# Hybrid RWKV-7 and attention layer: the block inverses work on a compact tile that ScalarE gathers, with one transposition in place of four

## The chip, the cores and the metric

The kernel runs on one core of one Trainium2 chip. The metric is device time in microseconds of one execution; the lower the better. The engines are named as in the profile: PE (TensorE, with PEld its weight loads), DVE (VectorE), ACT (ScalarE), POOL (GpSimd) and SP (SyncE, which here only issues DMAs). Each serves its own instructions in order.

## What is computed

One layer of a streaming encoder, on 512 prompt tokens and 32 sample tokens: a joint input projection, differential attention beside RWKV-7 time mixing, a merge with an output projection, and a gated ConvFFN. The part that matters here is the RWKV-7 recurrence, in the reference a loop over tokens:

```python
def step(S, inp):
    r_t, w_t, k_t, v_t, kk_t, a_t = inp
    sa = jnp.einsum('bhvk,bhk->bhv', S, -kk_t)
    S = (S * w_t[:, :, None, :] + sa[..., None] * (kk_t * a_t)[:, :, None, :]
         + v_t[..., None] * k_t[:, :, None, :])
    y = jnp.einsum('bhvk,bhk->bhv', S, r_t)
    return S, y
```

There are 16 heads of 64 values. The kernel does it in chunks of 64 tokens. Inside a chunk the tokens depend on each other through a unit triangular 64x64 matrix per head and chunk, and its inverse is needed before the chunks can be walked through.

## The kernel before

All large products are dense projections. `dense_g` (L222) makes one output tile of 128 columns: weights come by DMA in pieces of 128x512 (`load_w`, L212: L217 the DMA into one of three raw buffers `wr`, L218 the cast to `wh` on ACT, L219 the rest `wl` on DVE or POOL), and three matmuls of 272 columns per piece of 128 rows go into a PSUM tile `psd`. In the first stage these projections (first those that the recurrence needs, then fillers for the attention and the gates) fill TensorE between the small steps of the recurrence.

`Flow.run` (L106) puts the streams into one program: generators yield a time of a rough TensorE clock at which they want to go on, and dense work is taken while none is ready. Behind it a scheduler with costs of its own sets the final order on each engine, so a change of durations in the program text moves instructions far beyond the lines that it touches. The order on an engine is fixed when the program is built.

The streams of the first stage are:
- `elementwise` (L1059): per pair of heads, the decay and key terms (`rw_rates`, `rw_elem`, with norm products over `bonesr` into PSUM tiles `misc`, emptied by L565 and L587), stored to DRAM as `ar_d` and `bk_d`;
- `recurrence` (L1064): for each of two groups of four pairs, `rw_super` (L659) and then `rw_chain` (L720), which walks through the 8 chunks;
- `norms` (L1071) behind each chain (`rw_norm`, L841, with L867 and L871 emptying PSUM), `rw_sample` (L918) for the sample tokens, and `rotary`.

Behind these comes the attention (`attention`, L1297), with what is left of the fillers and the next projections as dense work beside it, and then dense stages to the end.

`rw_super` works on 32 small matrices for each of two heads. For each pair `chunk_products` (L615) makes the products and masks them into `mt` (L626), a tile of 128 partitions x 2 heads x 32 matrices x 128 columns. The 32x32 diagonal blocks lie in four quadrants of 32 partitions, each at a head and a column offset of its own; `QUADS` (L606) lists them. In turn:
1. L675: DVE transposes each quadrant's blocks into `NP` (a 32x32 blockwise transposition of 32x1024 elements), four instructions;
2. `inverse` (L480): 15 steps of a triangular inverse on the 16x16 diagonal blocks, two DVE instructions each, over 128 partitions, result in `Xp`;
3. `join16` (L631) joins 16x16 to 32x32 blocks: L635 transposes four quadrants of `Xp` into `NP`; `spread` (L680) transposes four quadrants of `Xp` to their places in `XT`; 128 matmuls, L645 empties them on ACT, 128 more, and L656 puts the result into `XT` on ACT and DVE in turn;
4. the join of 32x32 to 64x64 blocks: L688 transposes two quadrants of `XT` into `NP`, 64 matmuls, L698 empties them, 64 more, L708 puts them into `XT`.

`rw_chain` reads `mt` and `XT`. Its `load` (L728) brings `arL` and `bkL`, two buffers each, which `load_arbk` (L608) uses for the products too. A tile of such a name that is asked for takes the oldest buffer, and whatever writes it waits for the last reader of the tile before. `misc` has two PSUM buffers that all these steps share.

Of the kernel before, what the change touches and what calls it, by code (L numbers as in the profile page):

```python
# [10 lines left out]
F32 = mybir.dt.float32  # L11
# [15 lines left out]
SEQ = 512  # L27
# [9 lines left out]
SUP = 4  # L37
C = 64
NC = SEQ // C
# [122 lines left out]
def tile_hybrid_layer(  # L162
# [25 lines left out]
    V, A, G = nc.vector, nc.scalar, nc.gpsimd  # L188
    PE = Issue(tc, nc.tensor)
# [170 lines left out]
    rs, ms, rt = [npool.tile([128, TOK], F32, name=n) for n in ("rs", "ms", "rt")]  # L360
# [13 lines left out]
    for k in range(KT):  # L374
# [14 lines left out]
        for t in range(2):  # L389
            wh, wl = ws[t]  # L390
            for hf, (c0, c1) in enumerate(HALVES):
                for ip, (w, x) in enumerate(((wh, xg_h), (wh, xg_l), (wl, xg_h))):
                    PE.matmul(pj[t][hf][:, :c1 - c0], w[:, k % WK, :], x[:, k, c0:c1],
                              start=(k == 0 and ip == 0), stop=(k == KT - 1 and ip == 2))
# [59 lines left out]
    rp = ph1.enter_context(tc.tile_pool(name="rp", bufs=1, reuse_waits="tile"))  # L454
# [4 lines left out]
    def misc():  # L459
        return psm.tile([128, 512], F32, name="misc")  # L460


    mt = rp.tile([128, 2, 32, 128], F32, name="mt")
    XT = rp.tile([128, 32, 64], F32, name="XT")
# [5 lines left out]
    Xp = Xf[:, 0:1024].rearrange("p (a i) -> p a i", i=32)  # L470
    G.memset(XT, 0.0)

    def diag16(flat):

        return flat.rearrange("p (u x) -> p u x", u=2)[:, :, 0:512].rearrange("p u (a w) -> p u a w", w=32)[:, :, :, 0:16]

    def new_np():
        return rp.tile([128, 1056], F32, name="NP")

    def inverse(npf):  # L480

        X, N = diag16(Xf), diag16(npf)
        for i in range(1, 16):
            if i == 1:
                V.tensor_copy(out=X[:, :, 0, 1], in_=N[:, :, 1, 0])
                continue
            tmp = rp.tile([128, 512], F32, name="itmp")
            tv = tmp[:, :2 * i * i].rearrange("p (u a j) -> p u a j", u=2, a=i)
            V.tensor_tensor(out=tv, in0=X[:, :, 0:i, 0:i],
                            in1=N[:, :, i, 0:i].unsqueeze(2).to_broadcast([128, 2, i, i]), op=ALU.mult)  # L490
            V.tensor_reduce(out=X[:, :, 0:i, i], in_=tv, axis=AX.X, op=ALU.add)
# [114 lines left out]
    QUADS = [(32 * b + 64 * (1 - h), b, h) for h in range(2) for b in range(2)]  # L606

    def load_arbk(p):  # L608
        a = rp.tile([128, 2, SEQ], F32, name="arL", bufs=2)
        b = rp.tile([128, NC, 2, C], F32, name="bkL", bufs=2)  # L610
        nc.sync.dma_start(out=a, in_=ar_d[p, :, :, 0:SEQ])
        nc.sync.dma_start(out=b, in_=bk_d[p])
        return a, b

    def chunk_products(dst, m0, a, b):  # L615

        for q in range(NC // 4):
            pm = [misc(), misc()]
            for i in range(4):
                c = 4 * q + i  # L620
                for h in range(2):
                    f = slice(h * 64, h * 64 + 64)
                    PE.matmul(pm[h][:, i * 128:(i + 1) * 128], b[f, c, :, :].rearrange("p a t -> p (a t)"),
                              a[f, :, c * C:(c + 1) * C], start=True, stop=True)
            for h in range(2):
                V.tensor_tensor(out=dst[:, h, m0 + 4 * q:m0 + 4 * q + 4, :],  # L626
                                in0=pm[h].rearrange("p (m k) -> p m k", m=4),
                                in1=mask.unsqueeze(1).to_broadcast([128, 4, 128]), op=ALU.mult)
            yield PE.now + 2.0

    def join16(rows, src, M, xt, wait, spread):  # L631

        xz = new_np()[:, 0:512].rearrange("p (m a) -> p m a", m=32)
        for r0 in rows:
            V.transpose(out=xz[r0:r0 + 32].rearrange("p m a -> p a m"), in_=Xp[r0:r0 + 32, 0:16, :])  # L635
        spread()
        yield PE.now + wait
        ps = misc()
        for m in range(M):
            for q, r0 in enumerate(rows):  # L640
                PE.matmul(ps[r0:r0 + 32, m * 16:(m + 1) * 16], src(q, m), xz[r0:r0 + 32, m, :], start=True, stop=True)
        w = rp.tile([128, 512], F32, name="itmp")
        n = M * 16
        if len(rows) == 4:
            A.copy(out=w[:, :n], in_=ps[:, :n])  # L645
        else:
            for r0 in rows:
                A.copy(out=w[r0:r0 + 32, :n], in_=ps[r0:r0 + 32, :n])
        yield PE.now + 1.2
        ps = misc()  # L650
        for m in range(M):
            for q, r0 in enumerate(rows):
                PE.matmul(ps[r0:r0 + 16, m * 16:(m + 1) * 16], w[r0:r0 + 32, m * 16:(m + 1) * 16],
                          xt(q, slice(r0, r0 + 32))[:, m, 16:32], start=True, stop=True)
        for q, r0 in enumerate(rows):
            (V.tensor_copy if q % 2 else A.copy)(out=xt(q, slice(r0, r0 + 16))[:, 0:M, 16:32],  # L656
                                                 in_=ps[r0:r0 + 16, :n].rearrange("p (m k) -> p m k", m=M))

    def rw_super(s):  # L659
        p0 = s * SUP  # L660
        ab = {}
        for jj in range(SUP):
            yield ("out", p0 + jj), 0.0
            for k in range(jj, min(jj + 2, SUP)):
                if k not in ab and ("out", p0 + k) in flow.done:
                    ab[k] = load_arbk(p0 + k)
            yield max(PE.now + (4.0 if jj == 0 else 0.0), flow.done["out", p0 + jj] + 12.0)
            yield from chunk_products(mt, jj * NC, *ab[jj])
        yield from lock()


        with tc.high_priority(offset=1500):
            npf = new_np()
            for r0, b, h in QUADS:
                V.transpose(out=npf[r0:r0 + 32, 0:1024],  # L675
                            in_=mt[r0:r0 + 32, h, :, 32 * b:32 * b + 32].rearrange("p m t -> p t m"))
            inverse(npf)
        def spread():
            for r0, b, h in QUADS:
                V.transpose(out=XT[r0:r0 + 32, :, 32 * b:32 * b + 32].rearrange("p m i -> p i m"),  # L680
                            in_=Xp[r0:r0 + 32].rearrange("p a i -> p i a"))
        yield from join16(
            [q[0] for q in QUADS],
            lambda q, m: mt[QUADS[q][0]:QUADS[q][0] + 32, QUADS[q][2], m, 32 * QUADS[q][1]:32 * QUADS[q][1] + 32], 32,
            lambda q, r: XT[r, :, 32 * QUADS[q][1]:32 * QUADS[q][1] + 32], 28.0, spread)
        xz = new_np()[:, 0:1024].rearrange("p (m a) -> p m a", m=32)
        for r0 in (0, 64):
            V.transpose(out=xz[r0:r0 + 32], in_=XT[r0:r0 + 32, :, 0:32])  # L688
        yield PE.now + 7.0
        for m0 in (0, 16):  # L690
            ps = misc()
            for m in range(m0, m0 + 16):
                for h in range(2):
                    r0 = 64 * (1 - h)
                    PE.matmul(ps[r0 + 32:r0 + 64, (m - m0) * 32:(m - m0 + 1) * 32], mt[r0:r0 + 32, h, m, 32:64],
                              xz[r0:r0 + 32, m, :], start=True, stop=True)
            for r0, e in ((0, A.copy), (64, V.tensor_copy)):
                e(out=xz[r0 + 32:r0 + 64, m0:m0 + 16, :], in_=ps[r0 + 32:r0 + 64].rearrange("p (m k) -> p m k", m=16))  # L698
        yield PE.now + 1.5
        for m0 in (0, 16):  # L700
            ps = misc()
            for m in range(m0, m0 + 16):
                for h in range(2):
                    r0 = 64 * (1 - h)
                    PE.matmul(ps[r0:r0 + 32, (m - m0) * 32:(m - m0 + 1) * 32], xz[r0 + 32:r0 + 64, m, :],
                              XT[r0 + 32:r0 + 64, m, 32:64], start=True, stop=True)
            for r0, e in ((0, A.copy), (64, V.tensor_copy)):
                e(out=XT[r0:r0 + 32, m0:m0 + 16, 32:64], in_=ps[r0:r0 + 32].rearrange("p (m k) -> p m k", m=16))  # L708
        unlock()

    def lock():

        while flow.lock is not None:
            yield PE.now + 0.5
        flow.lock = True

    def unlock():
        flow.lock = None
# [199 lines left out]
    def rw_sample():  # L918
# [50 lines left out]
        def spread():  # L969
            V.transpose(out=xts.rearrange("p m i -> p i m"), in_=Xp.rearrange("p a i -> p i a"))  # L970
        yield from join16([0, 64], lambda q, m: mts[B[q], m, 0:32], 8, lambda q, r: xts[r], 26.0, spread)
        unlock()
        yield PE.now + 1.0
# [442 lines left out]
    with tc.tile_pool(name="op", bufs=1) as op:  # L1416
# [16 lines left out]
        ms, rt = [op.tile([128, TOK], F32, name=n) for n in ("ms", "rt")]  # L1433
# [11 lines left out]
    with tc.tile_pool(name="up", bufs=1) as up:  # L1445
# [11 lines left out]
        for f in range(FT):  # L1457
            cc = []
            for i in range(2):
                t = 2 * f + i  # L1460
# [23 lines left out]
    with tc.tile_pool(name="yp", bufs=1) as yp, tc.tile_pool(name="wlast", bufs=6, side="right") as wlast:  # L1484
        x2 = yp.tile([128, KT, TOK], F32, name="x2")
        acc = yp.tile([128, TOK], F32, name="acc")
        ms, rt, rs2 = [yp.tile([128, TOK], F32, name=n) for n in ("ms", "rt", "rs2")]
# [181 lines left out]
```

## Time and profile before

| | |
|---|---|
| median of 3 runs | 1366.93 us (1361.94 to 1367.68) |
| the profiled execution, its own time | 1367.84 us |
| its span, first to last instruction | 1366.0 us |
| mean granted TensorE clock over the span | 0.952 of 2.4 GHz |
| PE, PEld busy | 93%, 88% |
| DVE, ACT, POOL busy | 63%, 42%, 17% |
| first and second inverse, from L675 to the end of the joins | 210 to 288 us, 413 to 472 us |

The profile is one execution. A row of the trace gives the start, the duration, the engine, the line, the operation and the tiles (out<-in), and in brackets how long the engine had stood idle and which instruction released it. The share of busy time is a mean over stages with different limits, so the rows of the stage itself are read, and within it the wait that ends last. A TensorE row's busy time overlaps with the next one's, so the rate of dense matmuls is read from their starts.

### The profile page before, as it was taken

Reading aid. Unit: us, or ns where it says so; the run is one execution under the profiler, and the core shown is the slowest. Engines: PE = TensorE matmul, PEld = TensorE weight load, DVE = VectorE, ACT = ScalarE, POOL = GpSimd, SP = SyncE. Lnnn points to the kernel's source line nnn. Section 1 sums busy time; section 2 is a strip of 40 time slices with the busy share of each in tenths; the row PEclk is TensorE's granted clock in tenths of the full one; section 3 lists DMA queues with packets and bytes.
Section 4 is the critical chain, followed back from the end, with each engine's and each line's share of the span. In section 5 each row is a group of like instructions: output and inputs, shape, how many; then the busy total and the mean of one; then the engine's idle time right before and its main releaser. Section 6 shows DMA issues by size and latency. Waiting matters only on the chain. (4 is left out here: it accounts for less than half of the span.)

```text
span 1366.0 us, 29766 instructions
## 1 busy us (share of the span) xinstructions
PE 1264.7 (93%) x12014; PEld 1201.0 (88%) x12014; DVE 860.2 (63%) x1742; ACT 575.9 (42%) x1168; POOL 229.1 (17%) x264
## 2 busy tenths in 40 slices
PE   8798998799989899999987997999999999999996
PEld 7698988688878899988775895999999999999996
DVE  6857669855679333753456666566787777873323
ACT  5555454464412233332454555334544444453220
POOL 6600102111223101222221110000111111111111
PEclk9899898899989899999998998999999999999998
DMA  5254565144676253526776563345222222234321
GB/s 174 77 163 146 151 206 156 64 145 135 200 232 199 76 152 118 173 94 208 223 206 187 152 169 95 102 153 166 86 91 87 86 90 89 86 116 137 102 79 66
DMA packets 140329, 185.75 MB, mean 136 GB/s; under 512 B 42016, under 2 KB 65184, under 8 KB 140192
## 3 DMA queue, kind: packets, MB, share of 16 engines
q1 hardware_dynamic: 127120, 162.60, 39.9%
q10 hardware_dynamic: 13072, 21.26, 4.7%
q8 instruction: 94, 1.54, 0.5%
q14 instruction: 43, 0.35, 0.1%
HBM read 133.54 MB, written 37.41 MB: 125 GB/s over the span
## 5 line engine op out<-in xcount | busy, mean ns | idle before, releaser
L218 ACT CAST wh<-wr 128x512 fp32r<-128x512 f32 (+1 forms) x316 | 192.4, 615 | 374.2 <-PE psd L88 322.7
L88 PE MATMUL psd<-h_h,wh 128*128 128x272 f32 x976 | 299.5, 307 | 5.0 <-ACT qt L888 4.7
L88 PE MATMUL psd<-h_h,wl 128*128 128x272 f32 x976 | 291.7, 300 | 2.0 <-POOL wl L219 2.0
L88 PE MATMUL psd<-h_l,wh 128*128 128x272 f32 x976 | 292.7, 300 | 0.2 <-DVE h_l L443 0.2
L219 DVE TENSOR_TENSOR wl<-wr,wh 128x512 fp32r<-128x512 f32 x230 | 158.4, 693 | 116.9 <-ACT wh L218 111.9
L88 PEld LDWEIGHTS psd<-h_h,wh 128*128 128x128 f32 x976 | 192.9, 198 | 12.7 <-ACT qt L888 5.6
L88 PE MATMUL psd<-xgh,wl 128*128 128x272 f32 x704 | 203.9, 290 | 0.0
L88 PE MATMUL psd<-xgl,wh 128*128 128x272 f32 x704 | 203.3, 289 | 0.0
L88 PE MATMUL psd<-xgh,wh 128*128 128x272 f32 x704 | 202.1, 287 | 0.0
L88 PEld LDWEIGHTS psd<-h_h,wl 128*128 128x128 f32 x976 | 192.6, 198 | 4.3 <-POOL wl L219 2.5
L88 PEld LDWEIGHTS psd<-h_l,wh 128*128 128x128 f32 x976 | 193.2, 198 | 2.9 <-issue 1.4
L219 POOL TENSOR_TENSOR wl<-wr,wh 128x512 fp32r<-128x512 f32 x86 | 120.1, 1401 | 399.6 <-ACT wh L218 335.4
L88 PEld LDWEIGHTS psd<-xgl,wh 128*128 128x128 f32 x704 | 132.6, 188 | 0.0
L88 PEld LDWEIGHTS psd<-xgh,wl 128*128 128x128 f32 x704 | 132.4, 188 | 0.0
L88 PEld LDWEIGHTS psd<-xgh,wh 128*128 128x128 f32 x704 | 132.1, 188 | 0.1
L88 PE MATMUL psd<-ah,wh 128*128 128x272 f32 x352 | 101.7, 289 | 0.0
L88 PE MATMUL psd<-ah,wl 128*128 128x272 f32 x352 | 101.5, 288 | 0.0
L88 PE MATMUL psd<-al,wh 128*128 128x272 f32 x352 | 101.4, 288 | 0.0
L88 PE MATMUL psd<-ml,wh 128*128 128x272 f32 x256 | 74.6, 291 | 0.9 <-POOL ml L1134 0.9
L88 PE MATMUL psd<-mh,wh 128*128 128x272 f32 x256 | 74.8, 293 | 0.5 <-ACT mh L1133 0.4
L88 PE MATMUL psd<-mh,wl 128*128 128x272 f32 x256 | 74.6, 292 | 0.0
L1467 POOL COPY cvo<-uf 128x2 f32<-128x2 f32 x88 | 37.0, 452 | 220.6 <-DVE uf L1464 220.6
(369 smaller groups left out, 2537.5 us busy)
## 6 DMA issues: line engine op xcount, KB each, us to landing
wr<-w_in SPq DMA_DIRECT2D x132, 256.0 KB, 3.2
wr<-w_up SPq DMA_DIRECT2D x88, 256.0 KB, 2.8
wr<-w_down SPq DMA_DIRECT2D x40, 256.0 KB, 2.7
bkL<-bk_d SPq DMA_DIRECT2D x16, 512.0 KB, 5.2
ar_d<-ar SPq DMA_DIRECT2D x8, 544.0 KB, 3.2
t_d<-qt ACTq DMA_DIRECT2D x16, 272.0 KB, 3.4
bk_d<-bk SPq DMA_DIRECT2D x32, 128.0 KB, 3.1
arL<-ar_d SPq DMA_DIRECT2D x8, 512.0 KB, 4.7
```

The costliest lines, as they stand in the source:

```text
L88: ins = self.pe.matmul(out, lhsT, rhs, **kw)
L218: A.copy(out=wh[:, :n], in_=raw)
L219: le.tensor_tensor(out=wl[:, :n], in0=raw, in1=wh[:, :n].bitcast(F32), op=ALU.subtract)
L1467: G.tensor_copy(out=cvo[:, t, :, w], in_=u[:, 512 + w::32])
```

## The change

DVE's transpositions of four quadrants become one instruction over 128 partitions each. For that the diagonal blocks have to lie side by side at the same column offsets, so ACT copies them out of `mt` into a compact tile `dg` (in a buffer of `bkL`): after the third pair for three pairs (32x768 per quadrant), after the fourth for the last (32x256). The result goes into a compact tile `xd` (in a buffer of `arL`), the joins read and write it there, and ACT copies the diagonal blocks from it to `XT` (32x1024 per quadrant). The times that the planner is given are shorter. `rw_sample` uses `join16` too.

```diff
     def join16(rows, src, M, xt, wait, spread):
         xz = new_np()[:, 0:512].rearrange("p (m a) -> p m a", m=32)
-        for r0 in rows:
-            V.transpose(out=xz[r0:r0 + 32].rearrange("p m a -> p a m"), in_=Xp[r0:r0 + 32, 0:16, :])
+        V.transpose(out=xz.rearrange("p m a -> p a m"), in_=Xp[:, 0:16, :])
         spread()
...
             yield from chunk_products(mt, jj * NC, *ab[jj])
+            if jj == SUP - 2:
+                dg = rp.tile([128, NC, 2, C], F32, name="bkL", bufs=2).rearrange("p c a t -> p (c a t)")
+                dg = dg.rearrange("p (m t) -> p m t", t=32)
+            if jj >= SUP - 2:
+
+                ms = slice(0, (jj + 1) * NC) if jj == SUP - 2 else slice(jj * NC, (jj + 1) * NC)
+                for r0, b, h in QUADS:
+                    A.copy(out=dg[r0:r0 + 32, ms, :], in_=mt[r0:r0 + 32, h, ms, 32 * b:32 * b + 32])
         yield from lock()
...
             npf = new_np()
-            for r0, b, h in QUADS:
-                V.transpose(out=npf[r0:r0 + 32, 0:1024],
-                            in_=mt[r0:r0 + 32, h, :, 32 * b:32 * b + 32].rearrange("p m t -> p t m"))
+            V.transpose(out=npf[:, 0:1024], in_=dg.rearrange("p m t -> p t m"))
             inverse(npf)
+        xd = rp.tile([128, 2, SEQ], F32, name="arL", bufs=2).rearrange("p a t -> p (a t)")
+        xd = xd.rearrange("p (m i) -> p m i", i=32)
+
         def spread():
-            for r0, b, h in QUADS:
-                V.transpose(out=XT[r0:r0 + 32, :, 32 * b:32 * b + 32].rearrange("p m i -> p i m"),
-                            in_=Xp[r0:r0 + 32].rearrange("p a i -> p i a"))
+            V.transpose(out=xd.rearrange("p m i -> p i m"), in_=Xp.rearrange("p a i -> p i a"))
...
-            lambda q, r: XT[r, :, 32 * QUADS[q][1]:32 * QUADS[q][1] + 32], 28.0, spread)
+            lambda q, r: xd[r], 20.0, spread)
         xz = new_np()[:, 0:1024].rearrange("p (m a) -> p m a", m=32)
-        for r0 in (0, 64):
-            V.transpose(out=xz[r0:r0 + 32], in_=XT[r0:r0 + 32, :, 0:32])
-        yield PE.now + 7.0
+        V.transpose(out=xz, in_=xd)
+        for r0, b, h in QUADS:
+            A.copy(out=XT[r0:r0 + 32, :, 32 * b:32 * b + 32], in_=xd[r0:r0 + 32])
+        yield PE.now + 4.0
...
-                              XT[r0 + 32:r0 + 64, m, 32:64], start=True, stop=True)
+                              xd[r0 + 32:r0 + 64, m, :], start=True, stop=True)
```

The lines of the changed kernel are numbered otherwise: the gathers are L675 (to `dg`, shown as bkL) and L695 (to `XT`), the transpositions L681, L634, L687 (into `xd`, shown as arL) and L693, and L644, L655, L705 and L715 answer to L645, L656, L698 and L708.

The order of the instructions moves with it. First DVE at the end of the first inverse, before:

```order
L489 TENSOR_TENSOR itmp<-Xp,NP 128x450
L252 TENSOR_TENSOR lwl<-ss_2557,lwh 128x256
L491 TENSOR_REDUCE Xp<-itmp 128x2x15
L635 STREAM_TRANSPOSE NP<-Xp 32x16x32 x4
L680 STREAM_TRANSPOSE XT<-Xp 32x32x32 x4
L525 TENSOR_SCALAR tw<-tw 128x544
L565 TENSOR_SCALAR ss_2706<-misc 128x272
```

The same place of the changed kernel:

```order
L491 TENSOR_REDUCE Xp<-itmp 128x2x15
L252 TENSOR_TENSOR lwl<-ss_2558,lwh 128x256
L634 STREAM_TRANSPOSE NP<-Xp 128x16x32
L687 STREAM_TRANSPOSE arL<-Xp 128x32x32
L525 TENSOR_SCALAR tw<-tw 128x544
L526 SCALAR_TENSOR_TENSOR cs<-rmask,tw 128x544
L219 TENSOR_TENSOR wl<-wr,wh 128x512 x2
L350 COPY nsh<-u_100 128x2
L351 SCALAR_TENSOR_TENSOR r<-u_100,par,r 128x544
L352 TENSOR_SCALAR r<-u_100,der 128x1
L565 TENSOR_SCALAR ss_2838<-misc 128x272
L655 COPY arL<-misc 16x32x16
```

Eight transpositions between the inverse and L525 have become two, and L565, which empties a norm product, now stands further back, beside L655. On TensorE that norm product (`misc<-rn,bonesr`) stood ahead of the first join and now stands behind the second set of 16x16 matmuls.

Then ACT in the joins of the first group, in the changed kernel:

```order
L655 COPY arL<-misc 16x32x16
L695 COPY XT<-arL 32x32x32
L655 COPY arL<-misc 16x32x16
L695 COPY XT<-arL 32x32x32 x3
L570 ACT_TABLE_LOAD
L570 ACTIVATE rn<-ss_2838 128x544
L705 COPY NP<-misc 32x512
L256 ACTIVATE ssx<-rn 128x544
L705 COPY NP<-misc 32x512
```

The four L695 are new; a table load and an activation of `elementwise`, which before stood ahead of L645, now stand between them and L705.

Last SP behind the first inverse, in the changed kernel (each `arL` row of four is one load of the chain):

```order
L432 DMA vr_d<-vv 128x544
L741 DMA arL<-ar_d 128x2x128 x4
L217 DMA wr<-w_in 128x512 x5
L741 DMA arL<-ar_d 128x2x128 x4
L599 DMA ar_d<-ar 128x1088
L603 DMA bk_d<-bk 512x1x64 x2
```

Before, both loads of `arL` stood some ten rows further ahead, before the stores of the pair before. The second now stands behind five weight loads.

Counted over TensorE's whole order, the dense matmuls (into `psd`) that stand between the last chunk product of the second group and the first join are 193 before and 125 now, and ahead of the attention's first transposition (`tp<-cst,vt`) 2782 before and 2682 now. Between the low-rank matmuls ahead of the first group's last products stood 15, which now stand elsewhere; 22 stand between the two sets of 32x32 matmuls of the first group.

## Rows read from the trace of the kernel before

**Rows 1.** The page, busy time of each engine (us, share of the span, instructions).

```profile
PE 1264.7 (93%) x12014; PEld 1201.0 (88%) x12014; DVE 860.2 (63%) x1742; ACT 575.9 (42%) x1168; POOL 229.1 (17%) x264
```

**Rows 2.** Busy us per stretch: PE, PEld, DVE, ACT, POOL; clock, DMA share, GB/s.

```profile
212.00:244.00 32.00, 28.16 (x188) 27.05 (x189) 29.46 (x59) 10.67 (x21) 3.45 (x3) 0.86 0.54 156
244.00:260.00 16.00, 9.80 (x282) 9.18 (x285) 15.89 (x16) 8.38 (x15) 4.86 (x5) 0.84 0.14 43
260.00:276.00 16.00, 13.62 (x349) 13.29 (x342) 9.01 (x16) 6.58 (x13) 1.28 (x1) 0.73 0.13 43
```

**Rows 3.** DVE's transpositions by line: ns min/median/max, first and last start, form.

```profile
L635 DVE STREAM_TRANSPOSE NP<-Xp x10: 1064/1074/1093, 242.2 to 582.9; 32x512 f32<-32x512 f32 x10
L675 DVE STREAM_TRANSPOSE NP<-mt x8: 1892/2008/2047, 210.0 to 418.8; 32x1024 f32<-32x1024 f32 x8
L680 DVE STREAM_TRANSPOSE XT<-Xp x8: 1897/1960/2120, 246.6 to 447.4; 32x1024 f32<-32x1024 f32 x8
L688 DVE STREAM_TRANSPOSE NP<-XT x4: 1232/1234/1235, 275.5 to 459.0; 32x1024 f32<-32x1024 f32 x4
L966 DVE STREAM_TRANSPOSE NP<-mt x1: 2031/2031/2031, 565.5 to 565.5; 128x1024 f32<-128x1024 f32 x1
```

**Rows 4.** DVE's timeline at both inverses: start us, us, instruction.

```profile
246.57 8.03 DVE L680 STREAM_TRANSPOSE XT<-Xp 32x1024 f32<-32x1024 f32 x4
254.99 0.43 DVE L565 TENSOR_SCALAR ss<-misc 128x272 f32<-128x272 f32 x1
...
412.74 7.99 DVE L675 STREAM_TRANSPOSE NP<-mt 32x1024 f32<-32x1024 f32 x4
420.76 0.75 DVE L867 SCALAR_TENSOR_TENSOR vC<-misc,der,vC 128x512 f32<-128x512 f32 x1
...
436.83 4.41 DVE L635 STREAM_TRANSPOSE NP<-Xp 32x512 f32<-32x512 f32 x4
441.27 8.03 DVE L680 STREAM_TRANSPOSE XT<-Xp 32x1024 f32<-32x1024 f32 x4
```

**Rows 5.** PE's timeline: two waits and the first and last slow dense matmul behind each.

```profile
255.48 2.85 PE L88 MATMUL misc<-NP,mt 32*32 32x16 f32 x194 [4.47 <-DVE ss L565]
...
260.83 0.43 PE L88 MATMUL psd<-h_l,wh 128*128 128x272 f32 x1
...
264.92 0.43 PE L88 MATMUL psd<-h_l,wh 128*128 128x272 f32 x1
...
421.56 0.66 PE L92 MATMUL misc<-cst,ysb 128*128 128x128 f32 x4 [2.94 <-DVE vC L867]
...
422.35 0.43 PE L88 MATMUL psd<-h_h,wl 128*128 128x272 f32 x1
...
425.30 0.43 PE L88 MATMUL psd<-h_h,wh 128*128 128x272 f32 x1
```

**Rows 6.** Copies and activations between SBUF tiles: timelines of DVE and ACT, then L850.

```profile
254.63 0.44 DVE L525 TENSOR_SCALAR tw<-tw 128x544 f32<-128x544 f32 x1
256.65 0.66 ACT L528 ACTIVATE tw<-cs 128x544 f32<-128x544 f32 x1 [4.36 <-DVE cs L526]
L850 ACT ACTIVATE NP<-ysb x4: 1055/1056/1063, 372.9 to 591.8; 128x1024 f32<-128x1024 f32 x4
```

**Rows 7.** Stretches of the attention stage, and a dense stretch behind it (columns as rows 2).

```profile
700.00:720.00 20.00, 16.34 (x107) 16.08 (x108) 10.58 (x29) 12.40 (x36) 2.70 (x2) 0.83 0.75 205
730.00:760.00 30.00, 21.10 (x161) 15.93 (x161) 18.08 (x65) 15.73 (x53) 1.28 (x1) 0.77 0.64 183
884.00:918.00 34.00, 34.00 (x274) 34.00 (x273) 19.89 (x42) 11.78 (x22) 0.00 (x0) 1.00 0.50 156
```

**Rows 8.** DMA issues: out<-in, queue, count, KB each, median us from issue to landing.

```profile
wr<-w_in SPq DMA_DIRECT2D x132, 256.0 KB, 3.2
arL<-ar_d SPq DMA_DIRECT2D x32, 128.0 KB, 3.2
```

## The prediction

> **What bounds the kernel now.** I read the busy shares first, then the time around the two inverses engine by engine, then the waits there, then the attention stage. TensorE is busy for 93% of the span [rows 1], and nearly all of that is dense projection work which the change leaves alone. So a time can only fall where TensorE stands idle or runs at half clock. In the stretch of the first inverse VectorE is the full engine: 29.46 of 32 us, then 15.89 of 16 us, while ScalarE has 8.38 of those 16 us and TensorE 9.80 [rows 2]. What fills VectorE is to be seen next: the transposes of one quadrant of 32 partitions (512 or 1024 elements each) take 1.07, 2.01, 1.96 and 1.23 us, and the same form over all 128 partitions, in the sample's inverse, takes 2.03 us [rows 3]. The price goes by elements per partition; four quadrants one after the other pay it four times.
>
> Two TensorE waits come straight from that. In the first inverse the eight microseconds of L680 (246.57 to 254.60) stand in VectorE's queue ahead of L565, which empties a PSUM buffer, and the join matmuls wait 4.47 us for L565 [rows 4, 5]. In the second, the four L675 (412.74 to 420.73) stand ahead of L867, and TensorE waits 2.94 us for it [rows 4, 5]. Behind each wait a run of dense matmuls starts every 0.227 us: 19 from 260.83 to 264.92, 14 from 422.35 to 425.30 [rows 5]. In a stretch without waits one starts every 34/274 = 0.124 us [rows 7]. That is the lower clock level, 1.2 instead of 2.4 GHz; the granted clock averages 0.73 over 260 to 276 us [rows 2].
>
> **The change part by part.** The sum is made against the profiled execution, 1367.84 us, which is 0.9 us above the median of the three runs, 1366.93.
>
> *VectorE, per group of four pairs.* Four L675 become one: 4 x 2.01 - 2.03 = 6.0 us less. Four L635 become one: 3 x 1.07 = 3.2. Four L680 become one: 3 x 1.96 = 5.9. Two L688 become one: 1.2. Together 16.3 us, and 32.6 for both groups. For the forms that rows 3 do not show over 128 partitions I take the price of one quadrant; the upper bound is the 2.03 us of L966. The sample's join also loses one L635, 1.07 us, beside dense work: nothing.
>
> *ScalarE, per group.* Twelve copies are added: four of 32x768, four of 32x256, four of 32x1024. An activation over 544 elements takes 0.66 us and one over 1024 takes 1.06 us [rows 6], so by a line through both 0.84, 0.42 and 1.06: 9.3 us per group. The four 0.84 run before the last pair's products, and the four 1.06 beside the joins; only the four 0.42 = 1.7 us lie on the path from the last product to the inverse. From there to the first join the path gets shorter by 6.0 + 3.2 - 1.7 = 7.5 us.
>
> *A rule against this.* Between tiles in SBUF, 544 elements took 0.44 us on VectorE (L525) and 0.66 us on ScalarE (L528) [rows 6]. By that the gather would cost about 6 us on VectorE and costs 9 on ScalarE. The Trainium skill ("ScalarE: Activation LUTs", Rules for kernel authors) says to use VectorE for simple elementwise work, and the trace agrees about the single operation. It is still ScalarE that has room here [rows 2]; on VectorE the 6 us would come off the 16.3 saved, and the sum below would keep about two thirds of its first two terms.
>
> *TensorE, first group.* The order shows L565 behind one transposition instead of four, and the matmuls that L565 empties moved behind the first join. The wait of 4.47 us goes, and with it the matmuls at half clock behind it: 19 x 0.103 = 2.0 us. Together -6.5, bounds -6.5 and 0 (something else may hold the PSUM buffer). Late next is ScalarE in the joins: after its second L655 it has three 1.06 us copies, a table load and L570 ahead of L705, some 5 us, against the one-piece transposition and 22 dense matmuls on TensorE, some 5 us: +1, bounds 0 and +3. Ahead of the last products the order now runs the four low-rank groups without the 15 dense matmuls between them that covered ScalarE's evacuation: 15 x 0.124 = 1.9 us of cover gone, taken as +1.5, bounds 0 and +1.9.
>
> *TensorE, second group.* The 2.94 us go with the half-clock matmuls behind them, 14 x 0.103 = 1.4: -4.3, bounds -4.3 and 0. But the inverse runs from 420.76 to 441.27, 20.5 us of which L635 is 4.4 [rows 4], and is not shortened itself. From the last product to the join it will take some 1.7 + 2.0 + 15.4 + 1.1 + 1.5 (masks, handovers) = 21.7 us; TensorE has 125 dense matmuls there (193 before), 15.5 us, and about 4 us of norm work. New wait: +2, bounds 0 and +6; ScalarE's four small gathers stand behind two evacuations of dense results, hence the wide upper end.
>
> *What moves behind.* In the new order 2682 dense matmuls stand ahead of attention's first transposition, not 2782. These 100 x 0.124 = 12.4 us are not saved; they run later, beside attention. Attention has room: TensorE is idle 3.7 us of 700 to 720 and 8.9 of 730 to 760, and the clock means of 0.83 and 0.77 give away another 3.4 and 6.9 [rows 7]. Filled work is a gain up to 12.4 us, work queued ahead of attention's own chain is none: bounds -12.4 and 0. I take -5, nearer to none, since the waits there are a chain of softmax steps that dense work does not shorten.
>
> *Queues.* SP: the chain's second load of arL (four DMAs) now waits until the joins have read the buffer that xd took, and stands ahead of the next pair's stores and of weight loads. I cost it at nothing, as five weight loads stand ahead of it; without that cover it is the second rival. POOL: nothing is moved. ACT's own DMAs (z_d, q_d) go behind the gathers, up to 3 us later, and nobody waits for them in this stage.
>
> Sum: -6.5 + 1 + 1.5 - 4.3 + 2 - 5 = -11.3, so 1367.8 - 11.3 = 1356.5 for an execution like the profiled one, and 0.9 less for the median: **1356 us**, -0.8%. With all bounds on their good side -23.2, 1344; all on their bad side +10.9, 1378.
>
> **The rivals.**
> *No change that shows.* The dense matmuls moved behind are simply paid there (0 instead of -5), and the second inverse meets its new wait at +6: -2.3, so about 1365. For it: the 100 matmuls stay in the program. Against: half the room in 700 to 760 is idle that no dense work was left to fill.
> *ScalarE becomes the bound of the joins.* Its queue is served in order, and 9.3 us per group stand in front of weight casts and L705. Price: +3 instead of +1 in each group, and 2 us of half clock behind each: 2 x (3 + 2) - 1 = +9 on the sum, about 1365 too. It decides where TensorE waits for a cast (L218) or for L705. Against: 8.38 us of 16 in use [rows 2].
> *Slower: SP's queue is held.* If the arL load gets to the front of the queue before the joins have read xd, the weight loads behind it stop. A weight load takes 3.2 us to land [rows 8] and its cast about 0.6; with arL's own 3.2 us [rows 8] that is 7 us without weights per group, 2 us of half clock, and the chain's third chunk late by another 3: 2 x 12 = 24 on top of -11.3, so **about 1380**. It decides when more than the three raw weight buffers are used up before the last join. For it: the buffer was free of such a wait before. Against: the five weight loads that the order puts ahead.
> *The change does not do what it says*, should a transposition of one of these shapes over 128 partitions cost like four: no wait goes, and +1, +1.5 and +2 stay: about 1371. L966 speaks against it [rows 3].
>
> **How the numbers follow.** Forecast 0.55, no change 0.18, ScalarE 0.10, SP 0.14, price of the transposition 0.03. The forecast's own range is 1347 to 1363; with the others the range that should hold the time 8 times in 10 is 1344 to 1373, reaching over the two rivals at 1365 and leaving out most of the SP case and the very best ends. A measurement of this kernel can tell about 0.5% from no change, 6.8 us: faster means below 1360.1, slower above 1373.8. Faster: 0.85 of the forecast's chance and a quarter of that of the two rivals at 1365: 0.54. Slower: most of the SP case and a little of the rest: 0.15. Same: 0.31.
>
> **What would show it.** Each step right: the merged transpositions at about 1.1, 2.0, 2.0 and 1.2 us with 128 partitions; no wait of the first join for L565 and no wait for the first norm product behind the transpositions; TensorE's idle and half clock between 244 and 276 us smaller; the first attention transposition some 15 to 25 us earlier; less idle in attention's first three heads. Wrong: TensorE waits on L218 or L705 in the joins, a long wait of SP's arL load with casts waiting for weights, or attention that starts earlier and ends where it did.

## The result and the profile after

The changed kernel takes 1350.6 us (median of 4 runs, 1349.2 to 1353.9) against 1367.0 us before (4 runs): ratio 0.9888, 95% interval 0.9867 to 0.9909, a gain of 16.4 us where 11 were forecast. The profiled execution took 1350.93 us.

Busy time on the page of the changed kernel, against [rows 1]: VectorE has 29.8 us less and ScalarE 17.5 more.

```profile
PE 1257.4 (93%) x12014; PEld 1193.2 (88%) x12014; DVE 830.4 (62%) x1721; ACT 593.4 (44%) x1192; POOL 229.5 (17%) x264
```

Groups of instructions by line and shape, changed kernel (count, then busy us and mean ns, then idle before them), against [rows 3] and [rows 6]: one transposition over 128 partitions costs within 0.1 us what one quadrant did, and the copies have the prices of the line through the two activations.

```profile
L681 DVE STREAM_TRANSPOSE NP<-bkL 128x1024 f32<-128x1024 f32 x2 | 4.2, 2112 | 0.0
L687 DVE STREAM_TRANSPOSE arL<-Xp 128x1024 f32<-128x1024 f32 x2 | 4.1, 2046 | 0.0
L634 DVE STREAM_TRANSPOSE NP<-Xp 128x512 f32<-128x512 f32 x3 | 3.2, 1065 | 0.1
L693 DVE STREAM_TRANSPOSE NP<-arL 128x1024 f32<-128x1024 f32 x2 | 2.5, 1247 | 0.1
L695 ACT COPY XT<-arL 32x1024 f32<-32x1024 f32 x8 | 8.4, 1044 | 0.2
L675 ACT COPY bkL<-mt 32x768 f32<-32x768 f32 x8 | 6.6, 830 | 6.1 <-DVE mt L626 6.0
L675 ACT COPY bkL<-mt 32x256 f32<-32x256 f32 x8 | 3.2, 403 | 4.9 <-DVE mt L626 4.8
```

TensorE's timeline at the first joins and at the second inverse, changed kernel, against [rows 5]: the join no longer waits for the norm evacuation, but between its 512 small matmuls (256 in the program, each with two rows in the trace) TensorE now stands idle for 6.7 us for which the profile shows no releaser (its word is issue); and there are two waits that before had none like them, for a load of `lg` (4.86 us) and, as forecast, for the second inverse (1.44).

```profile
242.56 2.09 PE L88 MATMUL misc<-NP,mt 32*32 32x16 f32 x228
246.82 0.43 PE L88 MATMUL misc<-NP,mt 32*32 32x16 f32 x28 [2.16 <-issue]
...
250.37 1.26 PE L88 MATMUL misc<-arL,itmp 32*16 32x16 f32 x128 [1.28 <-issue]
254.92 0.45 PE L88 MATMUL misc<-arL,itmp 32*16 32x16 f32 x34 [3.29 <-issue]
...
413.94 2.04 PE L88 MATMUL misc<-sg,lg 128*128 128x512 f32 x2 [4.86 <-DMA lg<-lora]
432.30 2.14 PE L88 MATMUL misc<-NP,mt 32*32 32x16 f32 x175 [1.44 <-DVE NP L634]
```

To see where the time went I cut both executions at the same events: the last product of the first group, the last matmul of its joins, the last step of its chain, the last product of the second group, its first join, the first attention transposition, the last one that loads a head's values, the end. Columns as in [rows 2], the kernel before:

```profile
211.40:287.20 75.80, 62.22 (x1099) 59.50 (x1100) 63.32 (x102) 29.96 (x56) 11.50 (x10) 0.85 0.38 110
287.20:364.10 76.90, 75.28 (x1006) 65.63 (x1003) 44.61 (x102) 41.31 (x83) 11.80 (x12) 1.00 0.52 153
364.10:411.40 47.30, 41.88 (x339) 36.13 (x334) 36.18 (x71) 8.57 (x17) 10.62 (x7) 0.89 0.79 230
411.40:443.30 31.90, 28.96 (x208) 27.55 (x207) 29.49 (x45) 7.59 (x16) 10.40 (x9) 0.95 0.69 204
443.30:644.60 201.30, 190.30 (x2822) 178.76 (x2822) 91.80 (x182) 63.27 (x130) 34.41 (x28) 0.96 0.44 137
644.60:827.40 182.80, 160.98 (x1207) 143.31 (x1206) 109.38 (x341) 99.75 (x295) 33.37 (x25) 0.94 0.65 184
827.40:1366.00 538.60, 516.59 (x4039) 511.59 (x4037) 342.13 (x675) 205.66 (x349) 56.45 (x106) 0.98 0.33 101
```

and the changed kernel:

```profile
210.60:268.50 57.90, 47.76 (x1037) 46.18 (x1037) 41.34 (x81) 33.65 (x62) 9.98 (x9) 0.88 0.40 120
268.50:347.90 79.40, 78.28 (x1007) 66.80 (x1000) 44.56 (x102) 40.19 (x80) 10.58 (x12) 1.00 0.52 154
347.90:404.80 56.90, 51.79 (x395) 45.71 (x392) 43.88 (x83) 17.63 (x30) 11.51 (x9) 0.88 0.63 185
404.80:432.30 27.50, 21.21 (x137) 19.08 (x136) 21.47 (x43) 7.12 (x15) 7.34 (x6) 0.88 0.87 244
432.30:634.90 202.60, 191.25 (x2809) 179.16 (x2810) 87.02 (x176) 66.65 (x132) 36.46 (x28) 0.94 0.45 138
634.90:810.50 175.60, 165.15 (x1305) 149.66 (x1304) 109.13 (x340) 102.38 (x302) 37.60 (x28) 1.00 0.69 201
810.50:1349.10 538.60, 516.62 (x4042) 511.31 (x4040) 342.65 (x677) 205.92 (x351) 56.07 (x106) 0.98 0.32 102
```

The dense tail has not moved: 538.6 us in both. Attention is 7.2 us shorter although about 100 dense matmuls (12.4 us) more run in it: its idle time fell from 21.8 to 10.5 us and it is at the full clock throughout. Stage one is only 9.7 us shorter, although those 12.4 us have left it. So in this pair of profiles stage one lost 2.7 us on the same work and attention won 19.6, the reverse of the forecast's sum (-6.3 and -5). Two profiles are a thin ground for that: in a second execution of the changed kernel (run 3) the first attention transposition stands at 629.4 us and not at 634.9. Whether the shift from stage one to attention is the change's doing or that of the two planned waits that it also shortens (28 to 20 and 7 to 4 us) had to be tried.

### The profile page after: what moved, and what is told of

Read it like the earlier page. It is cut to its first block, busy times and chain, and to the rows that moved or that the text cites. A ratio compares the mean times of both kernels' runs of the same rounds, so it can differ in the third digit from the quotient of the medians.

```text
span 1349.1 us, 29750 instructions
## 1 busy us (share of the span) xinstructions
PE 1257.4 (93%) x12014; PEld 1193.2 (88%) x12014; DVE 830.4 (62%) x1721; ACT 593.4 (44%) x1192; POOL 229.5 (17%) x264
## 4 chain that ended last, share of the span: by engine, by line
PE 74%; DVE 11%; DMA 6%; ACT 4%; issue 3%; SPq 1%; POOL 1%; DVEq 0%; ACTq 0%
PE psd L88 59%; PE misc L88 6%; PE psq L88 3%; PE psy L88 2%; PE misc L92 2%; PE sc L88 1%; DMA raw<-q_d 1%; DMA raw<-k_d 1%; PE po L88 1%; PE tp L92 1%; SPq L1258 1%; DMA KH<-hi 1%; DMA Q<-raw 1%; ACT E L1294 1%; DVE itmp L489 1%
## 5 line engine op out<-in xcount | busy, mean ns | idle before, releaser
L218 ACT CAST wh<-wr 128x512 fp32r<-128x512 f32 (+1 forms) x316 | 192.5, 615 | 353.6 <-PE psd L88 302.3
L219 DVE TENSOR_TENSOR wl<-wr,wh 128x512 fp32r<-128x512 f32 x230 | 158.3, 692 | 107.3 <-ACT wh L218 100.7
L219 POOL TENSOR_TENSOR wl<-wr,wh 128x512 fp32r<-128x512 f32 x86 | 120.6, 1406 | 373.5 <-ACT wh L218 289.8
```

The costliest lines, as they stand in the source:

```text
L218: A.copy(out=wh[:, :n], in_=raw)
L219: le.tensor_tensor(out=wl[:, :n], in0=raw, in1=wh[:, :n].bitcast(F32), op=ALU.subtract)
```

## The experiments

How many dense matmuls stand ahead of attention's first transposition depends on the planned waits alone: 2782 with 28 and 7, 2682 with 20 and 4, whichever transpositions are used (their places within stage one differ a little). So the two parts can be tried crosswise. Ratios are to the kernel before, run beside them; in us I give them on 1367.

**1. The waits alone** (`before_w`).

```diff
-            lambda q, r: XT[r, :, 32 * QUADS[q][1]:32 * QUADS[q][1] + 32], 28.0, spread)
+            lambda q, r: XT[r, :, 32 * QUADS[q][1]:32 * QUADS[q][1] + 32], 20.0, spread)
...
-        yield PE.now + 7.0
+        yield PE.now + 4.0
```

> The kernel before with the two planned waits of the change (28 to 20 us ahead of the joins, 7 to 4 us ahead of the chunk joins) and nothing else: the 100 dense matmuls move from stage one to attention, VectorE keeps its 32.6 us of extra transposition time. Theory A (the gain needs both: dense work moved beside attention fills it, and the shorter transpositions let stage one do without that cover): attention gains as in the changed kernel, first to last load of a head's values 182.8 to about 176 us, but in stage one TensorE waits about 10 us longer per group for the inverse; about 1367, between 1361 and 1372. Rival B (the moved dense work is all of it): 1351, as the changed kernel. Rival C (VectorE's time is all of it, the moved work is paid where it goes): 1367 or more, with attention's own stretch longer by the 12.4 us that were moved.

Measured: 1363.0 us, ratio 0.9985 (0.9961 to 1.0008). Attention takes 179.2 us in its profile, stage one 642.8. The moved matmuls win 3.6 us there and in stage one 1.8 us remain of their 12.4; the dense tail is 3.5 us longer in this execution (542.1 us), so that its span is only 1.9 us shorter. Attention's stretch, and TensorE's waits for the first transposition behind the inverse (8.6 us at the second group's first join, 1.2 at the first group's; us, times, longest):

```profile
642.80:822.00 179.20, 166.89 (x1304) 151.14 (x1303) 109.29 (x340) 102.58 (x302) 37.60 (x28) 0.99 0.69 198
```

```profile
PE misc L88 <- DVE NP L635: 9.8, 3, 8.6
```

Rival B falls. The time allows A and C, but C's other condition failed: attention is shorter, not 12.4 us longer. A's wait of some 10 us per group came in the second group alone.

**2. The change with the old waits** (`after_w`).

```diff
-            lambda q, r: xd[r], 20.0, spread)
+            lambda q, r: xd[r], 28.0, spread)
...
-        yield PE.now + 4.0
+        yield PE.now + 7.0
```

> The changed kernel with the two planned waits of before (28 and 7 us): merged transpositions and gathers stay, 2782 dense matmuls stand in stage one as before. Theory A: attention as before (first to last load of values about 183 us), stage one shorter by the waits for the norm buffer and the first norm product that are gone, 5 to 10 us; about 1360, between 1356 and 1364. Rival B: 1367, as before. Rival C: 1351, as the changed kernel.

Measured: 1346.7 us, ratio 0.9866 (0.9828 to 0.9904), which is rival C's number (1348.7 on 1367, interval 1343.5 to 1353.9) and better than A's 1356 to 1364. All of the gain is there without moving anything to attention. Its stretches, cut at the same events up to the end of attention's loads:

```profile
211.80:275.60 63.80, 53.50 (x1084) 51.11 (x1082) 48.73 (x95) 36.71 (x69) 10.92 (x10) 0.89 0.48 141
275.60:347.60 72.00, 71.63 (x988) 64.30 (x983) 44.78 (x104) 41.62 (x81) 8.70 (x11) 1.00 0.52 151
347.60:388.40 40.80, 38.25 (x352) 33.65 (x347) 31.68 (x65) 12.38 (x21) 9.02 (x7) 1.00 0.84 255
388.40:420.10 31.70, 30.79 (x239) 29.34 (x239) 24.69 (x44) 9.57 (x21) 11.27 (x11) 1.00 0.78 242
420.10:623.60 203.50, 190.69 (x2823) 178.50 (x2823) 83.40 (x176) 67.69 (x134) 35.36 (x28) 0.96 0.45 138
623.60:803.50 179.90, 158.96 (x1207) 141.27 (x1206) 109.55 (x340) 99.62 (x295) 33.42 (x25) 0.96 0.66 187
```

Stage one is 21.0 us shorter than before on the same matmuls. By the rows, 12.0 come from the stretch of the first inverse (idle 13.6 to 10.3 us, clock 0.85 to 0.89, and some matmuls that run later), 4.9 from that of the first chain (idle 1.6 to 0.4, and again some matmuls that run later) and 6.5 from that of the second group's products (idle 5.4 to 2.6, clock 0.89 to 1.00). Beside these rows the changed kernel's third stretch is 16.1 us longer for about 44 dense matmuls (5.5 us) more: there stand the wait for `lg` and one of 3.7 us for L861, at a clock of 0.88. The second execution of the changed kernel has both waits too, 3.5 and 3.7 us. TensorE's waits in stage one of the changed kernel (us in total, times, longest us):

```profile
PE misc L88 <- DMA lg<-lora: 4.9, 1, 4.9
PE misc L92 <- DVE ysb L861: 4.1, 2, 3.7
...
PE misc L88 <- ACT tw L518: 2.0, 2, 1.8
```

**3. The changed kernel again** (`after_again`), to have it beside versions with the old waits.

> The changed kernel itself once more, beside the versions below. So far the shorter planned waits move 100 dense matmuls from stage one to attention and the time stands still (before with them 0.9985, the changed kernel without them 0.9866). Theory A (the moved cover is paid in stage one for what it fills in attention): 1348 to 1353, no faster than the changed kernel with the old waits, whose median was 1346.7. Rival D (the shorter waits are part of the gain, and the old waits' 1346.7 was chance): at least 3 us faster than the versions with old waits.

Measured: 1347.3 us, ratio 0.9892 (0.9862 to 0.9923). With 0.9866 for the old waits, the shorter waits are worth nothing that shows. Rival D, which asked for 3 us less than with old waits, falls. This run's theory A (paid in stage one for what it fills in attention) is what the stretches of both executions show: against run 2 attention is 4.3 and 5.1 us shorter, stage one 11.3 and 5.8 us longer. Attention here:

```profile
629.40:804.20 174.80, 165.30 (x1305) 149.65 (x1304) 109.00 (x340) 102.50 (x302) 37.59 (x28) 1.00 0.71 202
```

**4. Only the part ahead of the inverse** (`first_half`): gathers and L681 as changed, the joins of before, the changed kernel's waits. The cut is against the changed kernel.

```diff
-            V.transpose(out=xd.rearrange("p m i -> p i m"), in_=Xp.rearrange("p a i -> p i a"))
+            for r0, b, h in QUADS:
+                V.transpose(out=XT[r0:r0 + 32, :, 32 * b:32 * b + 32].rearrange("p m i -> p i m"),
+                            in_=Xp[r0:r0 + 32].rearrange("p a i -> p i a"))
...
```

> The changed kernel with the gathers and the one merged transposition ahead of the inverse, but the joins of before (four transpositions each over 32 partitions, joins on the wide tile); the planned waits are the changed kernel's. It saves 6.0 - 1.7 us per group on the path ahead of the inverse and leaves 10.3 us per group on VectorE in the joins. Theory A: attention gains in full, the eight transpositions of the joins stand again in front of the norm evacuation, so TensorE waits some 4 us per group more than in the changed kernel; about 1358, between 1354 and 1362. Rival B: 1351. Rival C: 1350 plus two thirds of what the changed kernel gained: about 1361.

Measured: 1352.0 us, ratio 0.9907 (0.9879 to 0.9935). On 1367 that is 1354.3 (1350.5 to 1358.1): at the lower edge of what A said (1354 to 1362), and C's 1361 falls.

**5. Only the joins** (`joins_only`): no gathers, four L675 as before, the changed kernel's waits.

```diff
-            V.transpose(out=npf[:, 0:1024], in_=dg.rearrange("p m t -> p t m"))
+            for r0, b, h in QUADS:
+                V.transpose(out=npf[r0:r0 + 32, 0:1024],
+                            in_=mt[r0:r0 + 32, h, :, 32 * b:32 * b + 32].rearrange("p m t -> p t m"))
...
```

> The changed kernel with the joins on the compact tile, but the four transpositions over 32 partitions ahead of the inverse and no gathers; planned waits as in the changed kernel. VectorE has 6.0 us per group more than in the changed kernel, ScalarE 5.1 us less. Theory A: the inverse starts 4.3 us later per group, so the wait of the join for the inverse (1.4 us in the second group) grows by about 4 us; about 1356, between 1352 and 1361. Rival B: 1351. Rival C: 1350 plus one third of the gain: about 1356 too.

Measured: 1358.9 us, ratio 0.9970 (0.9943 to 0.9997). On 1367 that is 1362.9 (1359.2 to 1366.6), less than the 11 us that both theories gave the joins. With the part ahead of the inverse -12.7 us (-17 to -9), with the joins alone -4.1 (-8 to -0.4): about three quarters of the gain are ahead of the inverse, though only 6 of VectorE's 16.3 us per group are. So VectorE's time does not count by its sum. Nor does TensorE's wait for the second inverse decide: it is 8.6 us in run 1, 5.7 in run 4 and 3.9 in run 5, all with the same planned waits, and run 4 is the faster. The second group's first join in runs 1, 4 and 5:

```profile
441.45 0.25 PE L88 MATMUL misc<-NP,mt 32*32 32x16 f32 x2 [8.57 <-DVE NP L635]
426.34 0.26 PE L88 MATMUL misc<-NP,mt 32*32 32x16 f32 x2 [5.74 <-DVE NP L635]
439.64 2.28 PE L88 MATMUL misc<-NP,mt 32*32 32x16 f32 x155 [3.89 <-DVE NP L634]
```

**6. The second group alone** (`second_only`) **and 7. the first alone** (`first_only`), with old waits.

The code of both kernels stands under a condition, `s == 1` or `s == 0`:

```diff
+            if s == 1:
+                V.transpose(out=npf[:, 0:1024], in_=dg.rearrange("p m t -> p t m"))
+            for r0, b, h in [] if s == 1 else QUADS:
+                V.transpose(out=npf[r0:r0 + 32, 0:1024],
+                            in_=mt[r0:r0 + 32, h, :, 32 * b:32 * b + 32].rearrange("p m t -> p t m"))
...
```

> Old planned waits; the gathers, the merged transpositions and the compact joins in the second group of four pairs alone, the first group as before. In the run with both groups changed and old waits, the time to the same dense matmul was that of before up to the 1600th (+3.5 us) and 23 us ahead from the 1900th on: all of the gain lies between 345 and 436 us, in the second group. Theory E (it comes from the second group's own VectorE time, 16.3 us): about 1347 as with both groups. Rival F (the first group's shorter transpositions bring the first chain and the second group's products forward, and that is the gain): about 1362 to 1366.

> Old planned waits; the change in the first group of four pairs alone, the second group as before. The order of the matmuls is that of the version with both groups (the second group's products stand 48 to 66 dense matmuls earlier than before). Theory E: 1362 to 1366, as before. Rival F: about 1347 to 1352, most of the gain.

Measured: the second alone 1360.3 us, ratio 0.9969 (0.9943 to 0.9996); the first alone 1346.9 us, ratio 0.9888 (0.9854 to 0.9922). Theory E falls. In us, -4.2 and -15.3, and together -19.5 against -18.3 for both. The times at which some events start, from the timelines (in brackets the dense matmuls ahead of them, counted in the same rows with the first projections, 72 more than in the order), show why the gain had seemed to lie in the second group:

| | before | second alone | first alone | both |
|---|---|---|---|---|
| last join matmul, first group | 287.2 (1420) | 286.1 (1420) | 275.9 (1392) | 275.6 (1392) |
| last step of its chain | 364.1 (1631) | 364.5 (1631) | 347.9 (1599) | 347.6 (1599) |
| last product, second group | 411.4 (1766) | 412.1 (1766) | 393.0 (1740) | 388.4 (1740) |
| first join, second group | 443.3 (1959) | 439.3 (1959) | 430.8 (1959) | 420.1 (1959) |

The first group's joins end 11.3 us earlier, with 28 fewer dense matmuls (3.5 us) ahead of them. The chain, the norms and the second group's products come forward with them, and 18 us stand there at the last product. Less the dense matmuls that are still to run, at 0.124 us each, the first alone is ahead by 7.8 us at the last join matmul, 12.2 at the last step of the chain and 15.2 at the last product: about half of the lead is made behind the joins. Aligned by dense matmuls alone, as I had read it, the chain's steps that were already done did not count. The profiled execution of the first alone, 1355.5 us, was the longest of its six, so its last row understates it. Each version also has an order of its own, from the scheduler; the new order with the long transpositions was not run, so how much of the gain is VectorE's time and how much the order that comes with it is not shown.

**8. A cover that is not needed** (`sample18`), on the changed kernel with old waits.

```diff
-        yield from join16([0, 64], lambda q, m: mts[B[q], m, 0:32], 8, lambda q, r: xts[r], 26.0, spread)
+        yield from join16([0, 64], lambda q, m: mts[B[q], m, 0:32], 8, lambda q, r: xts[r], 18.0, spread)
```

> The changed kernel with the old planned waits (28 and 7), and the planned wait ahead of the sample's join cut from 26 to 18 us: 52 dense matmuls (6.5 us) move from the sample's stretch to attention. There the join stood 7.7 us behind its transposition (560.5 and 568.2 us in the run with the old waits), so that this cover is not needed, and attention has 20.9 us of idle TensorE. Theory A: no new wait and 4 to 6 us off, 1341 to 1343. Rival (moved dense work is always paid where it goes): 1347, no change.

Measured: 1336.0 us, ratio 0.9787 (0.9757 to 0.9818), more than expected. Stage one loses 4.6 us and attention 3.2 against `after_w`, with 52 dense matmuls changing places. TensorE waits 0.29 us for the transposition, and has 12.6 us of idle time left in attention; its timeline and attention's stretch:

```profile
564.52 0.68 PE L88 MATMUL misc<-NP,mt 32*32 32x16 f32 x32 [0.29 <-DVE NP L634]
```

```profile
619.00:795.70 176.70, 164.10 (x1261) 145.25 (x1259) 107.36 (x341) 101.56 (x299) 35.75 (x27) 0.98 0.68 197
```

**9. The same cut on the kernel before** (`before_s18`): 26 to 18 in the same line.

> The kernel before with nothing but the planned wait ahead of the sample's join cut from 26 to 18 us (52 dense matmuls, 6.5 us, go from the sample's stretch to attention). A control for the version that had this cut on top of the changed kernel with its old waits and ran at 0.9787 against 0.9866 without the cut. If the cut is worth the same by itself (the cover was not needed there, attention had idle time for it): about 0.8% below before, 1353 to 1358. If it needs the shorter transpositions: 1362 to 1366.

Measured: 1357.8 us, ratio 0.9942 (0.9918 to 0.9967). The cut is worth 8 us (4.5 to 11) by itself and does not need the transpositions.

**10. Past the point** (`sample14`): 14 instead of 18 in the same line.

> The changed kernel with old waits and the sample's wait at 14 us. With 18 us the join came 0.3 us after its transposition was ready, so no cover is left to take. Of the 44 dense matmuls that move on, 22 stood ahead of the join. Theory A (cover that is needed is paid for): TensorE waits 2 to 4 us for the transposition L634 there, and the time is that of 18 us or up to 4 us above, 1336 to 1340. Rival (dense work moved to attention is always a gain): another 3 to 5 us off, 1331 to 1333.

Measured: 1334.1 us, ratio 0.9767 (0.9744 to 0.9790). The wait is there, as the waits of TensorE in the sample's stretch show, but the time is no longer for it:

```profile
PE misc L88 <- DVE NP L634: 3.0, 1, 3.0
```

The number lies between the two theories and cannot be told from that of 18 us. It is the fastest version, 2.3% below before.

**11. The copies on VectorE** (`copies_dve`) **and 12. on ScalarE, made twice** (`copies_twice`), with old waits. The cut shows run 11; in run 12 each `A.copy` line that it takes out stands twice.

```diff
-                    A.copy(out=dg[r0:r0 + 32, ms, :], in_=mt[r0:r0 + 32, h, ms, 32 * b:32 * b + 32])
+                    V.tensor_copy(out=dg[r0:r0 + 32, ms, :], in_=mt[r0:r0 + 32, h, ms, 32 * b:32 * b + 32])
...
-            A.copy(out=XT[r0:r0 + 32, :, 32 * b:32 * b + 32], in_=xd[r0:r0 + 32])
+            V.tensor_copy(out=XT[r0:r0 + 32, :, 32 * b:32 * b + 32], in_=xd[r0:r0 + 32])
```

> The changed kernel with old waits (1346.7) and its twelve copies per group on VectorE instead of ScalarE. By the row of L525 (544 elements in 0.44 us) they cost VectorE some 6 us per group, ScalarE loses 9.3. If VectorE's queue is what counts, about a third of the gain goes: 1350 to 1356. If the copies' place on the path counts, where VectorE does each in less time: 1343 to 1347. This is the choice of engine that the Trainium skill ("ScalarE: Activation LUTs", Rules for kernel authors) speaks for.

> The changed kernel with old waits and each of the twelve copies per group made twice, on ScalarE: 9.3 us more of ScalarE per group. If ScalarE has room there, as its 8.38 of 16 us ahead of the joins said, nothing changes but the 1.7 us of small gathers per group on the path: 1347 to 1351. If ScalarE is the bound of the joins (a rival of the prediction: 3 us and 2 us of half clock per group): 1355 to 1360.

Measured: on VectorE 1350.9 us, ratio 0.9895 (0.9863 to 0.9926); twice on ScalarE 1347.5 us, ratio 0.9870 (0.9847 to 0.9894), the time of once. So another 9 us of ScalarE per group cost nothing that shows (the interval is 3 us to either side). The instructions of L695 on VectorE take 0.69 us where ScalarE takes 1.04 (above):

```profile
L695 DVE COPY XT<-arL x8: 681/685/690, 267.9 to 445.8; 32x1024 f32<-32x1024 f32 x8
```

The Trainium skill ("ScalarE: Activation LUTs", Rules for kernel authors) sends `relu`, `max`, `min`, `add` and `mul` to VectorE and does not list a plain copy. For the copy, too, VectorE is the faster here by the row above, and still the version that has it there is no faster. Its first group's joins end at 283.3 us instead of 275.6 (both with old waits), with 14 more dense matmuls ahead of them, but the intervals of the two versions overlap, so that it is slower is not shown.

## Why the prediction was right, and where its steps were not

The sum came out within its range by errors of opposite sign that partly cancel, so that its nearness is in part luck.

- **Price of the transpositions:** right, 2.11, 1.07, 2.05 and 1.25 us (L681, L634, L687, L693). VectorE lost 29.8 us of busy time. The rival that the change does not do what it says falls.
- **First group, "-6.5 + 1 + 1.5":** the step that failed. The wait for L565 went and the uncovered low-rank term came (a wait of 1.8 us for `tw`), but the first group alone brings -15.3 us (-20 to -11) where these terms give -4. I priced one wait and the half-clock matmuls behind it, 6.5 us from [rows 5], and not that everything behind the inverse starts earlier: by the end of the joins the stretch with both groups changed is 12.0 us shorter, and at the second group's last product run 7 has 18. What I named as late next, ScalarE, costs nothing that shows (run 12); what stands there instead is 6.7 us between TensorE's small matmuls from 242 to 255, without a releaser. How the rest divides between idle time and clock was not settled by a run of its own.
- **Second group, "-4.3 + 2":** right as far as it can be seen. Alone, with old waits and so without the new wait, it brings -4.2 (-7.8 to -0.5), against -4.3. The new wait for the inverse measured 1.44 in the changed kernel, where fewer dense matmuls cover it.
- **"-5" for the dense work moved beside attention:** wrong. The fill is real, 16.7 us in attention between the changed kernel and the version with old waits (179.9 to 175.6 us with 12.4 more in it), but the same matmuls were cover in stage one, which is 11.3 us longer without them (17.5 and 5.8 in the second execution). Runs 1 to 3 put the sum of both at nothing that shows. I counted what attention gains and left out what stage one loses; my rival "paid where they go" had the sign, not the place.
- **"First attention transposition 15 to 25 us earlier":** 9.7 us in the first profile of the changed kernel and 15.2 in the second, at the lower edge at best; right with the old waits, 21.0.
- **SP's queue:** the load did come to the front early, and waited 18.8 us in two pieces between 235 and 275 us; but from 195 to 290 us TensorE's waits for weights (L218, L219) are 1.2 us together, so the buffers lasted. In the second group the chain's load waited 4.5 us and TensorE waited for no weights from 425 to 490 us; the load of `lg` that was late is on the same queue, but no held load of the chain stood ahead of it. Of the rival's 12 us per group nothing came. A buffer of its own for `xd`, which would take the wait away, was not tried. SP's waits in that stretch of the changed kernel (us, times, longest):

```profile
SPq L741 <- DVE NP L693: 10.3, 1, 10.3
SPq L741 <- PE misc L88: 8.5, 1, 8.5
```

- **The copies on VectorE instead:** the forecast was that this would lose about a third; run 11's middle value loses a fifth (0.9895 against 0.9866), and the intervals overlap, so no loss is shown.

## What to carry to other kernels

Where dense work fills the gaps of a chain, price a shorter step by the time at which the chain's next events start, less the dense work that is still to run, and not by the one wait that goes. Dense work that covers a wait was paid for here where it was taken (runs 1 to 3), in spite of 21.8 us of idle time elsewhere, while cover longer than the wait it hides could go (runs 8 and 9): compare when the result is ready with when it is used. And when one edit shortens work and retunes the plan, run the two crosswise; here the retuning hid nothing and added nothing that shows, and a planned wait outside the change held 8 us.

## What the runs showed of the hardware

A transposition by VectorE over 128 partitions of 1024 elements, with one side rearranged, took 1.96 to 2.14 us (L681, L687), over 32 partitions 1.89 to 2.12 [rows 3]: the partitions are nearly free. Where neither side is rearranged (L693) it took 1.25 us over 128 partitions, and L688, over 32, took 1.23 [rows 3].

A second matter was not expected: between the 512 small matmuls of the first joins TensorE stood 6.7 us idle without a releaser in the changed kernel, where it had been 3.5 in the kernel before, whose timeline of TensorE shows there:

```profile
259.47 1.05 PE L88 MATMUL misc<-NP,mt 32*32 32x16 f32 x62 [1.14 <-issue]
...
270.08 0.89 PE L88 MATMUL misc<-XT,itmp 32*16 32x16 f32 x89 [2.38 <-issue]
```

These breaks stand at fixed places. Counted over all that the trace has of TensorE (matmuls, weight loads and its sequencer's own) from 0, they come ahead of number 3522 and 4034 before, and of 3521, 3778 and 4034 in the changed kernel: 256 apart or a multiple of it, to within one. It is so in the joins of every version here; 128 of these matmuls with their weight loads, the 256 of such a step, pass in some 1.3 us. What makes the engine stop there no trace shows. The breaks of the first joins come to 3.3 to 4.0 us in the three versions that still wait 4.4 to 4.5 us for L565 (the kernel before, the second group alone, run 9) and to 5.1 to 7.4 in the eight executions that have no wait there, with 3.9 to 5.2 in the three that have shorter waits; that the wait's going gives part of its time back to the breaks is argued from this, not shown.
